# The attention item loop of a two-layer decoder trunk: three engines in source order, and the background work in another order

## The chip, the cores and the metric

The kernel runs on one core of one Trainium2 chip. The metric is the device time of one execution in microseconds. The kernel before took 1172.36 us (median of three runs: 1175.97, 1169.79 and 1172.36). The changed kernel's time is to be compared with that.

## The reference, cut to what matters

A decoder trunk of two layers with S = 512 rows, D = 1024, 16 heads of 64 in 4 groups. Layer A is a short gated convolution and an MLP; then one shared key/value side is projected; layer B is native sparse attention on it, and an MLP. The change touches layer B's attention:

```python
kv = (h @ w_kv).reshape(B, S, 6, N_KV_GROUPS, HEAD_DIM)
k_raw, v_raw, k_sel, v_sel, k_win, v_win = (kv[:, :, i] for i in range(6))
k_cmp = compress_blocks(k_raw, cmp_pe_k, phi_k_w1, phi_k_w2)   # 31 tokens: silu(blocks @ w1) @ w2
v_cmp = compress_blocks(v_raw, cmp_pe_v, phi_v_w1, phi_v_w2)
...
def one_block(qb):                                             # 4 blocks of 128 queries
    o_c = softmax(qt . k_cmp + bias_c) @ v_cmp                 # compressed branch
    o_s = softmax(qt . k_sel + bias_s) @ v_sel                 # selection branch
    o_w = softmax(qt . k_win + bias_w) @ v_win                 # window branch
    return gt[..., 0:1] * o_c + gt[..., 1:2] * o_s + gt[..., 2:3] * o_w
...
x = x + o.reshape(B, S, N_HEADS * HEAD_DIM) @ w_o
x = x + squared_relu_mlp(rms_norm(x, norm_mlp[layer]), mlp_w1[layer], mlp_w2[layer])
```

With 512 rows and 8 selection blocks of 64, all causal blocks are selected and the window reaches over all rows, so both branches are plain causal attention here, each on its own keys and values.

## The kernel before, in words

**Products.** Every large matmul is done in fp16 with each operand split in a high and a low part, in three products (`mm3`, L341 to L343: hi x hi, hi x lo, lo x hi). Weights come from memory in pieces of 128 x 1024 by DMAs on SyncE's queue (`wst`), in the order of the list that begins at L100 and is built by `block` and `cols`; ScalarE makes `whi` (L195) and VectorE `wlo` (L196). `next_piece` takes the next one of the list, `ahead_fine` converts the following ones in steps of 512 columns between the matmuls.

**PSUM.** `bank(name)` gives accumulators in rotation: two each of a, b and c, one each of d and e. In the item loop background pieces use "a" (through `abank`), scores use "b", transposes, the compressed branch's outputs and the finish use "c", and "d" and "e" accumulate PV.

**Items.** The attention stage is a list of 96 items. `Full(g, qb, br, heads)` is one to four heads of group g for query block qb against the keys of one branch (0 selection, 1 window), and `Cmp(gp, qb)` eight heads of two groups against the compressed tokens. List A has the 44 items of groups 0 and 1; B has 22 of group 2 and four Cmp of groups 0 and 1; C has 22 of group 3 and the four Cmp of groups 2 and 3. `mixed(items, extra, start, step)` puts the first Cmp ahead of the item `start` of its list and the others each `step` items further. An item has five steps:
- `st0`: scores into a bank "b" (L954, L955); VectorE adds the bias, finds the row bound and copies to `at_s` (L962, a fused reduce); ScalarE takes exp into `at_p` (L964).
- `st1`: transposes of `at_p` into a bank "c" (L970); ScalarE writes the high part `at_ph` (L973).
- `st2`: VectorE writes the low part `at_pl` (L976).
- `st3`: PV in three products (L989 to L991); for the last head of a branch VectorE scales by the gate and the row sum (`rl`, `add_parts`, L894 and L898, `o_t`), POOL adds into `o` (L900, L903).
- `st4`: when all branches of a group and block are in, `finish` transposes `o` (L917) and splits it into the output operand, which lies in `big`.

`need()` names the background pieces that must be issued before the scores, `need3()` those before PV.

**Background.** A generator hands out the remaining projections in small portions between the items: values of the selection branch (v0), queries of group 1 (q1), keys and values of the window branch (k1, v1), q2, then `raw(0)`, `phi(0)` (compressed keys), `raw(1)`, `phi(1)` (compressed values, marked "cmp"), q3, and, when the outputs of groups 0 and 1 are there ("o1"), the half of the output projection that needs them. Each turn of the loop has a credit; a yield costs the number yielded (0.65 for six matmuls of 512 columns), or 0.1. `ensure(names)` runs the generator until a named piece is done, whatever the credit.
- `gated_pair` accumulates two banks "a" over eight weight slices. `queries` evicts them with L645 (VectorE), then ScalarE and POOL (L746, L747) write `Q`; `keys` evicts with L645 and writes `KD` four times per bank on ScalarE (L691) and VectorE (L693).
- `values` evicts four half banks with ScalarE and L716 on VectorE.
- `raw` evicts with L765 into `at_s`, splits it into `kr_hl` (L362 ScalarE, L364 VectorE; one buffer), and six DMAs per half copy that, shifted, into `big` (L771 to L773, SyncE's queue). `big` has one buffer.
- `phi` multiplies `big` by the first compression weights in 96 matmuls of 155 columns in all, goes through tanh and a multiplication (`phi_t`, L804 to L806, ScalarE and VectorE), splits into `phi_h`, and does a second, small product. For the values that product takes `phi_h` repeated into `kr_hl` (L828, L833) and is evicted into VC by L838 and a split.
- `out_proj` evicts with L469 into the residual `X`.

**Order.** Everything is written in source order, but the Tile scheduler decides the order in which each engine gets its instructions. The loop writes the steps of an item some turns apart:

```python
lead = {1: 2, 2: 3, 3: 4, 4: 6}
...
items[i].st0()
credit += 1.25 if "q3" not in done else 0.9
...                                             # background, while credit > 0
for s in (1, 2, 3, 4): j = i - lead[s]; ...     # st1 of item i-2, st2 of i-3, st3 of i-4, st4 of i-6
```

Before the loop a lead-in issues k0, q0 and the gates, with accumulators of its own choice (`acc`).

Of the kernel before, what the change touches and what calls it, by code (L numbers as in the profile page):

```python
# [10 lines left out]
F32 = mybir.dt.float32  # L11
# [37 lines left out]
def body(ctx, tc, x, rel_bias, norm_mix, norm_mlp, mlp_w1, mlp_w2, a_w_in, a_conv_w, a_w_out,  # L49
# [69 lines left out]
    block(w_kv, 1024)  # L119
    block(w_kv, 1280)  # L120
    block(b_w_qg[0], 512)
    block(w_kv, 0)
    block(phi_k_w1, 0, SW, 0, 16)
# [476 lines left out]
    with pool("attn") as ap:  # L600
# [153 lines left out]
        def raw(which):  # L754
# [7 lines left out]
            for m in range(2):  # L762
                t = ftile("at_s", 3)
                by_stride = lambda a: a.rearrange("p (b r) -> p r b", r=16)
                DVE.tensor_tensor(t.rearrange("p (r b) -> p r b", r=16), by_stride(po[m]), by_stride(rbk),  # L765
                                  op=OP.mult)
                hl = ap.tile([128, 4, S], F16, name="kr_hl", bufs=1)[:, 0:2]
                split_to(hl[:, 0], hl[:, 1], t)
                for s in range(2):
                    g, r = 2 * m + s, slice(64 * s, 64 * s + 64)  # L770
                    nc.sync.dma_start(kr[0:64, :, g, :], hl[r])  # L771
                    nc.sync.dma_start(kr[64:128, :, g, 0:S - 32], hl[r, :, 32:S])
                    nc.sync.dma_start(kr[64:128, :, g, S - 32:S - 1], hl[r, :, 1:32])  # L773
                yield
# [4 lines left out]
        def phi(which):  # L779
# [18 lines left out]
            for m in range(2):  # L798
                bias = ap.tile([128, 2], F32, name="phi_b", bufs=2)
                ACT.activation(bias[:, 0:1], ph[m][:, 124:125], AF.Copy)  # L800
                ACT.activation(bias[:, 1:2], ph[m][:, 124:125], AF.Copy, scale=0.5 / (SW * SK))
                t = ap.tile([128, G, 31], F32, name="phi_t", bufs=2)
                v = ph[m][:, 0:124].rearrange("p (g j) -> p g j", g=4)
# [7 lines left out]
            if which == 0:  # L811
                pk = bank("c")
                w2 = [ap.tile([128, 2, 2, 64], F16, name=f"phi_w2{i}") for i in range(2)]
                for i in range(2):
# [7 lines left out]
            else:  # L822
                pv = bank("c")
                hd = ap.tile([128, 4, S], F16, name="kr_hl", bufs=1).rearrange(
                    "p (m i) (g h n) -> p m i g h n", m=2, g=G, h=4)
                for m in range(2):
                    for i in range(2):
                        DVE.tensor_copy(hd[:, m, i], hs[:, m, i][:, :, None, :].to_broadcast([128, G, 4, 32]))  # L828
                for g in range(4):
                    o = pv[:, g * 64:(g + 1) * 64]  # L830
                    for m in range(2):
                        lh = [hd[:, m, i, g].rearrange("p h n -> p (h n)") for i in range(2)]
                        PE.matmul(o, lh[0], w[0][:, m], start=m == 0, stop=False)  # L833
                        PE.matmul(o, lh[0], w[1][:, m], start=False, stop=False)
                        PE.matmul(o, lh[1], w[0][:, m], start=False, stop=m == 1)
# [36 lines left out]

        for k in (keys(0), marked("q0", queries(0)), gates()):
            drain(k)
# [5 lines left out]
        def add_parts(g, n, qb, src, scale):  # L880


            if (g // 2, qb) not in og:
                og[g // 2, qb] = ap.tile([128, 2, 256], F32, name="o", bufs=6)
            dst = og[g // 2, qb][:, g % 2:g % 2 + n].rearrange("p g (h d) -> p (g h) d", d=64)
# [219 lines left out]
        A = branch(0, 0) + branch(1, 0) + branch(0, 1) + branch(1, 1)  # L1105
        B = mixed(both(2, (0, 1, 2, 3)), [Cmp(0, qb) for qb in range(4)], 10, 3)
        C = mixed(both(3, (3, 2, 1, 0)), [Cmp(1, qb) for qb in (3, 2, 1, 0)], 4, 4)
# [4 lines left out]
        def background():  # L1112
            yield from marked("v0", values(0))
            yield from marked("q1", queries(1))
            yield from marked("k1", keys(1))
            yield from marked("v1", values(1))
            yield from marked("q2", queries(2))
            yield from raw(0)
            yield from phi(0)
            yield from raw(1)  # L1120
            yield from marked("cmp", phi(1))
            yield from marked("q3", queries(3))
            while "o1" not in done:
                yield "wait"
            yield from out_proj(0)
# [8 lines left out]

        lead = {1: 2, 2: 3, 3: 4, 4: 6}
        credit = 0.0
        for i in range(len(items) + 6):
            if i < len(items):
                ensure(items[i].need())
                at_item.get(i, lambda: None)()  # L1140
                items[i].st0()
            credit += 1.25 if "q3" not in done else 0.9
            while credit > 0.0:
                u = next(bg, "end")
                if u in ("wait", "end"):
                    credit = 0.0
                else:
                    credit -= u or 0.1
            for s in (1, 2, 3, 4):
                j = i - lead[s]  # L1150
                if 0 <= j < len(items):
                    if s == 3:
                        ensure(items[j].need3())
                    getattr(items[j], f"st{s}")()
        for _ in bg:
# [147 lines left out]
```

## Time and profile before

| | us |
|---|---|
| median of three runs | 1172.36 |
| lowest, highest run | 1169.79, 1175.97 |
| profiled execution | 1169.18 |
| its span | 1167.4 |
| attention stage, as looked at below (524 to 831) | 307.0 |
| TensorE busy in it | 267.5 |
| VectorE, ScalarE, GpSimd busy in it | 235.7, 201.4, 44.5 |
| mean granted TensorE clock | 0.988 |

The profile is of one execution. PE is TensorE's matmuls, PEld its weight loads, DVE VectorE, ACT ScalarE, POOL GpSimd, SP SyncE. Names such as L976 are lines of the kernel before, and "out<-in" gives tiles by the program's names. A group of instructions has its count, its busy time, the mean duration of one in ns, then the idle time of its engine just before them and what ended it. "Waited for" rows tell, for one engine, the instruction that waited, the one that released it, the sum in us, how often, and the longest. Rows of time stretches give busy time and count for each engine, then the granted clock as a part of full speed, the share of the DMA engines' time, and GB/s.

### The profile page before, as it was taken

Reading aid. Unit: us, or ns where it says so; the run is one execution under the profiler, and the core shown is the slowest. Engines: PE = TensorE matmul, PEld = TensorE weight load, DVE = VectorE, ACT = ScalarE, POOL = GpSimd, SP = SyncE. Lnnn points to the kernel's source line nnn. Section 1 sums busy time; section 2 is a strip of 40 time slices with the busy share of each in tenths; the row PEclk is TensorE's granted clock in tenths of the full one; section 3 lists DMA queues with packets and bytes.
Section 4 is the critical chain, followed back from the end, with each engine's and each line's share of the span. In section 5 each row is a group of like instructions: output and inputs, shape, how many; then the busy total and the mean of one; then the engine's idle time right before and its main releaser. Section 6 shows DMA issues by size and latency. Waiting matters only on the chain.

```text
span 1167.4 us, 20139 instructions
## 1 busy us (share of the span) xinstructions
PE 1103.2 (95%) x7959; PEld 697.5 (60%) x7959; DVE 835.2 (72%) x1527; ACT 571.4 (49%) x924; POOL 159.1 (14%) x201
## 2 busy tenths in 40 slices
PE   9999999999999999998899759799999999999995
PEld 4444444447874468856576636566444688445884
DVE  5755568756986558987687837887976589754795
ACT  4523344444343444467677736665744443343352
POOL 0000001321001220001102000312043200022020
PEclk9999999999999999999999989999999999999998
DMA  6432336333333332242112533011543333330221
GB/s 204 128 104 95 108 98 185 96 109 109 109 110 108 108 98 93 72 129 77 51 56 77 150 89 108 3 53 58 161 128 91 109 113 105 109 108 19 73 91 73
DMA packets 149378, 115.75 MB, mean 99 GB/s; under 512 B 8612, under 2 KB 146564, under 8 KB 149284
## 3 DMA queue, kind: packets, MB, share of 16 engines
q1 hardware_dynamic: 146736, 109.47, 30.8%
q10 hardware_dynamic: 2260, 4.40, 1.2%
q8 instruction: 62, 1.02, 0.3%
q0 software_dynamic: 288, 0.61, 0.2%
q14 instruction: 32, 0.26, 0.1%
HBM read 110.22 MB, written 2.14 MB: 96 GB/s over the span
## 4 chain that ended last, share of the span: by engine, by line
PE 41%; DVE 22%; ACT 13%; issue 9%; POOL 8%; DMA 5%; SPq 1%; DVEq 0%; ACTq 0%; POOLq 0%
POOL ml_z L503 7%; DVE wlo L185 5%; PE a L341 5%; PE a L342 5%; PE a L343 5%; DMA wst<-mlp_w_dram 4%; ACT rh L504 4%; DVE wlo L196 3%; DVE wst L182 3%; DVE ml_t L499 3%; PE b L342 2%; PE b L341 2%; ACT ml_z L501 2%; PE b L343 2%; PE c L341 2%
## 5 line engine op out<-in xcount | busy, mean ns | idle before, releaser
L195 ACT ACTIVATE whi<-wst 128x1024 f16<-128x1024 f32 (+3 forms) x170 | 142.0, 860 | 142.6 <-PE a L342 48.8
L196 DVE SCALAR_TENSOR_TENSOR wlo<-wst,whi 128x1024 f16<-128x1024 f32 (+3 forms) x170 | 167.4, 992 | 54.6 <-ACT whi L195 54.4
L503 POOL TENSOR_TENSOR ml_z<-ml_z 128x256 f32<-128x256 f32 x128 | 102.6, 822 | 602.7 <-ACT ml_z L501 402.7
L341 PEld LDWEIGHTS <-whi 128*128 128x128 f16 x1024 | 101.0, 99 | 126.1 <-issue 16.4
L184 ACT ACTIVATE whi<-wst 128x1792 f16<-128x1792 f32 x64 | 106.8, 1691 | 131.8 <-DVE wst L182 103.1
L343 PEld LDWEIGHTS <-wlo 128*128 128x128 f16 x1024 | 100.7, 98 | 112.3 <-issue 0.8
L342 PEld LDWEIGHTS <-whi 128*128 128x128 f16 x1024 | 100.7, 98 | 107.0 <-issue 1.3
L505 DVE TENSOR_TENSOR rl<-ml_z,rh 128x1792 f16<-128x1792 f32 x32 | 64.8, 2025 | 139.2 <-ACT rh L504 139.2
L185 DVE SCALAR_TENSOR_TENSOR wlo<-wst,whi 128x1792 f16<-128x1792 f32 x64 | 129.4, 2027 | 2.9 <-ACT whi L184 2.9
L182 DVE TENSOR_TENSOR wst<-wst 128x256 f32<-128x256 f32 x256 | 107.0, 460 | 22.2 <-DMA wst<-mlp_w_dram 21.0
L504 ACT ACTIVATE rh<-ml_z 128x1792 f16<-128x1792 f32 x32 | 54.3, 1697 | 106.2 <-POOL ml_z L503 106.2
L552 PEld LDWEIGHTS <-wlo 128*128 128x128 f16 x896 | 87.6, 98 | 14.9 <-issue 3.9
L551 PEld LDWEIGHTS <-whi 128*128 128x128 f16 x896 | 87.6, 98 | 14.5 <-issue 4.0
L550 PEld LDWEIGHTS <-whi 128*128 128x128 f16 x896 | 87.6, 98 | 10.6
L964 ACT ACTIVATE at_p<-at_s,at_m 128x128 f32<-128x128 f32 (+3 forms) x128 | 70.9, 555 | 35.0 <-DVE at_m L962 34.6
L501 ACT ACTIVATE ml_z<-ml_t 128x1024 f32<-128x1024 f32 x32 | 33.8, 1056 | 88.3 <-DVE ml_t L499 88.3
L341 PE MATMUL a<-xsh,whi 128*128 128x512 f16 x192 | 72.8, 379 | 1.9 <-DVE phi_t L806 1.9
L551 PE MATMUL a<-rl,whi 128*128 128x256 f16 x256 | 69.8, 273 | 3.4 <-DVE rl L505 3.4
L341 PE MATMUL c<-xsh,whi 128*128 128x512 f16 x192 | 72.8, 379 | 0.0
L342 PE MATMUL c<-xsl,whi 128*128 128x512 f16 x192 | 72.8, 379 | 0.0
L343 PE MATMUL c<-xsh,wlo 128*128 128x512 f16 x192 | 72.8, 379 | 0.0
L343 PE MATMUL b<-xsh,wlo 128*128 128x512 f16 x192 | 72.8, 379 | 0.0
(309 smaller groups left out, 2719.9 us busy)
## 6 DMA issues: line engine op xcount, KB each, us to landing
wst<-mlp_w_dram SPq DMA_DIRECT2D x256, 256.0 KB, 3.3
wst<-a_w_in_dram SPq DMA_DIRECT2D x18, 512.0 KB, 3.5
wst<-w_kv_dram SPq DMA_DIRECT2D x12, 512.0 KB, 3.6
T<-ext_d ACTq DMA_DIRECT2D x4, 1056.0 KB, 5.3
wst<-a_w_out_dram SPq DMA_DIRECT2D x8, 512.0 KB, 3.4
wst<-b_w_qg_dram SPq DMA_DIRECT2D x8, 512.0 KB, 3.6
wst<-b_w_o_dram SPq DMA_DIRECT2D x8, 512.0 KB, 3.4
wst<-a_w_in_dram SPq DMA_DIRECT2D x8, 384.0 KB, 5.4
```

The source lines that it names most:

```text
L182: DVE.tensor_tensor(b[:, :, o], b[:, :, x], b[:, :, y], op=e)
L184: ACT.activation(hi, b[:, :, 1:], AF.Copy, scale=sc)
L185: DVE.scalar_tensor_tensor(lo, b[:, :, 1:], sc, hi, op0=OP.mult, op1=OP.subtract)
L195: ACT.activation(hi[:, s:e], w, AF.Copy, scale=sc)
L196: DVE.scalar_tensor_tensor(lo[:, s:e], w, sc, hi[:, s:e], op0=OP.mult, op1=OP.subtract)
L341: PE.matmul(ps, w[0], xs[0], start=start, stop=False)
L342: PE.matmul(ps, w[0], xs[1], start=False, stop=False)
L343: PE.matmul(ps, w[1], xs[0], start=False, stop=stop)
L503: POOL.tensor_tensor(z[:, o], z[:, a], z[:, b], op=e)
L504: ACT.activation(rh[0][:, p], z[:, 1:8], AF.Copy)
L550: PE.matmul(acc7[i], wh, xh, start=c == 0 and not other, stop=False, skip_group_check=other)
L551: PE.matmul(acc7[i], wh, xl, start=False, stop=False, skip_group_check=other)
```

## The change: three engines in source order, and the background rearranged

In words: (1) the loop stands in a block in which TensorE, ScalarE and VectorE take their instructions in the order of the source; GpSimd and SyncE are left to the scheduler. (2) Each turn writes finish of item i-6, PV of i-4, transposes of i-2, scores of i, low part of i-2, then background with credits of 1.3 and 0.85; before that it asks for what item i+2 needs. (3) v0 moves to the lead-in. (4) raw(0) comes ahead of q2 (with its weights, `block(w_kv, 0)`), and four turns without further background ("rest") stand between raw(1) and phi(1). (5) `kr_hl` has two buffers of half the size, and the copies of the second half of each pair go to GpSimd's queue. (6) The first Cmp stands at item 58 in place of 54, and they follow every third in place of every fourth. (7) `o` has seven buffers, paid with one buffer of `phi_t` and with tiles that the second compression product now takes from others.

```diff
@@ weights
+    block(w_kv, 0)
     block(b_w_qg[0], 512)
-    block(w_kv, 0)
@@ raw
-                hl = ap.tile([128, 4, S], F16, name="kr_hl", bufs=1)[:, 0:2]
+                hl = ap.tile([128, 2, S], F16, name="kr_hl", bufs=2)
                 split_to(hl[:, 0], hl[:, 1], t)
                 for s in range(2):
                     g, r = 2 * m + s, slice(64 * s, 64 * s + 64)
-                    nc.sync.dma_start(kr[0:64, :, g, :], hl[r])
-                    nc.sync.dma_start(kr[64:128, :, g, 0:S - 32], hl[r, :, 32:S])
-                    nc.sync.dma_start(kr[64:128, :, g, S - 32:S - 1], hl[r, :, 1:32])
+                    q = (nc.sync, nc.gpsimd)[s]
+                    q.dma_start(kr[0:64, :, g, :], hl[r])
+                    q.dma_start(kr[64:128, :, g, 0:S - 32], hl[r, :, 32:S])
+                    q.dma_start(kr[64:128, :, g, S - 32:S - 1], hl[r, :, 1:32])
@@ phi
-                t = ap.tile([128, G, 31], F32, name="phi_t", bufs=2)
+                t = ap.tile([128, G, 31], F32, name="phi_t", bufs=1)
...
-                w2 = [ap.tile([128, 2, 2, 64], F16, name=f"phi_w2{i}") for i in range(2)]
+                w2 = [ap.tile([128, S], F16, name=n, bufs=3)[:, 0:256].rearrange("p (m a b) -> p m a b", m=2, a=2)
+                      for n in ("at_ph", "at_pl")]
...
-                hd = ap.tile([128, 4, S], F16, name="kr_hl", bufs=1).rearrange(
-                    "p (m i) (g h n) -> p m i g h n", m=2, g=G, h=4)
+                hd = [ap.tile([128, 2, S], F16, name="kr_hl", bufs=2).rearrange(
+                    "p i (g h n) -> p i g h n", g=G, h=4) for _ in range(2)]
@@ lead-in, lists, background
-        for k in (keys(0), marked("q0", queries(0)), gates()):
+        for k in (keys(0), marked("q0", queries(0)), gates(), marked("v0", values(0))):
...
-                og[g // 2, qb] = ap.tile([128, 2, 256], F32, name="o", bufs=6)
+                og[g // 2, qb] = ap.tile([128, 2, 256], F32, name="o", bufs=7)
...
-        B = mixed(both(2, (0, 1, 2, 3)), [Cmp(0, qb) for qb in range(4)], 10, 3)
+        B = mixed(both(2, (0, 1, 2, 3)), [Cmp(0, qb) for qb in range(4)], 14, 2)
...
-            yield from marked("v0", values(0))
             yield from marked("q1", queries(1))
             yield from marked("k1", keys(1))
             yield from marked("v1", values(1))
+            yield from raw(0)
             yield from marked("q2", queries(2))
-            yield from raw(0)
             yield from phi(0)
             yield from raw(1)
+            for _ in range(4):
+                yield "rest"
             yield from marked("cmp", phi(1))
@@ the loop
-        lead = {1: 2, 2: 3, 3: 4, 4: 6}
-        for i in range(len(items) + 6):
-            if i < len(items):
-                ensure(items[i].need())
-                at_item.get(i, lambda: None)()
-                items[i].st0()
-            credit += 1.25 if "q3" not in done else 0.9
-            while credit > 0.0:
-                u = next(bg, "end")
-                if u in ("wait", "end"):
-                    credit = 0.0
-                else:
-                    credit -= u or 0.1
-            for s in (1, 2, 3, 4):
-                j = i - lead[s]
-                if 0 <= j < len(items):
-                    if s == 3:
-                        ensure(items[j].need3())
-                    getattr(items[j], f"st{s}")()
+        with tc.manual_schedule(engines={mybir.EngineType.PE, mybir.EngineType.Activation, mybir.EngineType.DVE}):
+            for i in range(len(items) + 6):
+                def step(n, k):
+                    if 0 <= i - k < len(items):
+                        it = items[i - k]
+                        if n == 3:
+                            ensure(it.need3())
+                        getattr(it, f"st{n}")()
+                if i < len(items):
+                    ensure(items[min(i + 2, len(items) - 1)].need())
+                    ensure(items[i].need())
+                    at_item.get(i, lambda: None)()
+                step(4, 6)
+                step(3, 4)
+                step(1, 2)
+                step(0, 0)
+                step(2, 2)
+                credit += 1.3 if "q3" not in done else 0.85
+                while credit > 0.0:
+                    u = next(bg, "end")
+                    if u in ("wait", "end", "rest"):
+                        credit = 0.0
+                    else:
+                        credit -= u or 0.1
```

More of the change, by code (lines that the diff above doesn't have):

```diff
@@ L823, in phi @@
                 pv = bank("c")
-                hd = ap.tile([128, 4, S], F16, name="kr_hl", bufs=1).rearrange(
-                    "p (m i) (g h n) -> p m i g h n", m=2, g=G, h=4)
+                hd = [ap.tile([128, 2, S], F16, name="kr_hl", bufs=2).rearrange(
+                    "p i (g h n) -> p i g h n", g=G, h=4) for _ in range(2)]
                 for m in range(2):
                     for i in range(2):
-                        DVE.tensor_copy(hd[:, m, i], hs[:, m, i][:, :, None, :].to_broadcast([128, G, 4, 32]))
+                        DVE.tensor_copy(hd[m][:, i], hs[:, m, i][:, :, None, :].to_broadcast([128, G, 4, 32]))
                 for g in range(4):
@@ L831, in phi @@
                     for m in range(2):
-                        lh = [hd[:, m, i, g].rearrange("p h n -> p (h n)") for i in range(2)]
+                        lh = [hd[m][:, i, g].rearrange("p h n -> p (h n)") for i in range(2)]
                         PE.matmul(o, lh[0], w[0][:, m], start=m == 0, stop=False)
```

## The prediction

> **What bounds the kernel now.** I read the page first, then the busy time by stage, then what TensorE waited for, last the groups of the engines that release it.
>
> ```profile
> PE 1103.2 (95%) x7959; PEld 697.5 (60%) x7959; DVE 835.2 (72%) x1527; ACT 571.4 (49%) x924; POOL 159.1 (14%) x201
> ```
>
> TensorE is busy for 95% of the profiled execution, so a change of order can only win back idle TensorE time. The diff touches the attention stage alone, 524 to 831 us. Busy time there (us, PE, PEld, DVE, ACT, POOL, each with its count; then granted clock, DMA share, GB/s):
>
> ```profile
> 524.00:535.00 11.00, 8.04 (x74) 6.32 (x72) 8.28 (x24) 9.45 (x22) 4.95 (x4) 1.00 0.15 49
> 535.00:560.00 25.00, 24.89 (x216) 16.65 (x214) 19.44 (x53) 17.73 (x46) 0.30 (x1) 1.00 0.28 86
> 560.00:567.00 7.00, 4.00 (x36) 2.12 (x35) 2.15 (x13) 3.85 (x11) 4.96 (x4) 1.00 0.23 75
> ...
> 640.00:660.00 20.00, 15.11 (x185) 11.21 (x184) 17.25 (x60) 15.47 (x50) 1.46 (x2) 0.91 0.50 134
> ...
> 684.00:699.00 15.00, 1.88 (x42) 1.66 (x41) 3.98 (x6) 2.35 (x4) 0.00 (x0) 0.68 0.44 105
> 699.00:728.00 29.00, 26.72 (x258) 19.33 (x256) 20.81 (x59) 16.60 (x45) 1.47 (x2) 0.93 0.29 92
> 728.00:757.00 29.00, 22.86 (x265) 16.75 (x266) 25.28 (x61) 20.17 (x45) 9.62 (x9) 0.94 0.06 19
> ...
> sum 307.00, PE 267.52 PEld 184.32 DVE 235.74 ACT 201.39 POOL 44.50; mean PE 20.58 PEld 14.18 DVE 18.13 ACT 15.49 POOL 3.42
> ```
>
> The stage holds 307.0 - 267.5 = 39.5 us of idle TensorE; nothing the change does can win more, the half clock (0.68 and 0.91 to 0.94) aside. VectorE, at 235.7 of 307, is next: 77% over the stage, 87% in 728 to 757. What the idle time waited for (us, times, longest):
>
> ```profile
> PE a L341 <- DMA big<-kr_hl: 13.1, 1, 13.1
> PE b L954 <- POOL Q L747: 4.7, 7, 1.1
> PE a L341 <- DVE phi_t L806: 3.7, 2, 1.9
> PE c L970 <- DVE at_pl L976: 3.7, 6, 1.7
> PE d L989 <- ACT at_ph L973: 3.2, 5, 1.4
> PE b L1027 <- DVE at_m L962: 2.0, 1, 2.0
> PE b L954 <- DVE at_m L962: 1.6, 2, 0.9
> ...
> PE a L341 <- DVE VT L716: 0.3, 1, 0.3
> ```
>
> One wait is a third of it: phi(1) cannot start before the raw copies have landed. The last row matters for what follows: today a projection that needs a bank just being evicted costs next to nothing, since items are pulled ahead of it.
>
> **The change part by part.** Gains first.
>
> Start of the loop: 524 to 535 idles 2.96 us. With v0 drained before the loop, its 96 matmuls run with nothing beside them but lose nothing (they depend only on weights), and Q of group 0 is older by them. I leave 1.0 us: -2.0. From 560 to 567 3.00 us are idle while POOL is busy for 4.96 of 7: the items of a group stand behind the Q that POOL is still writing. With items two slots ahead asked for early, the pair is finished sooner: -3.0.
>
> 640 to 660 idles 4.89 us, and its clock of 0.91 costs about 0.09 x 15.11 = 1.4 us more; VectorE is full there (17.25 of 20) because raw, a Cmp and conversions meet. Spread out, about 1.5 stay: -4.8.
>
> The at_pl, at_ph and at_m waits add up to 10.5 us in the rows above; some 6.5 lie in 640 to 660 and 728 to 757. With two slots between the steps the other 4 should vanish: -4.0. From 728 to 757 no background is left; 6.14 us are idle, but VectorE itself needs 25.28 of the 29, so 3.7 is the most: -2.0.
>
> The raw copies. The second half (m = 1) waited for the first half's copies, kr_hl being one buffer:
>
> ```profile
> 683.51 1.97 DVE L765 TENSOR_TENSOR at_s<-a,rb 128x512 f32<-128x512 f32 x2 [2.62 <-PE a L343]
> ...
> 686.76 0.60 SPq L771 DMA_DIRECT2D big<-kr_hl  x1
> ...
> 691.96 0.63 ACT L362 ACTIVATE kr_hl<-at_s 128x512 f16<-128x512 f32 x1 [6.24 <-DMA big<-kr_hl]
> ...
> 698.49 0.29 PE L341 MATMUL a<-big,whi 128*128 128x155 f16 x1 [13.12 <-DMA big<-kr_hl]
> ...
> 707.25 0.23 PE L343 MATMUL a<-big,wlo 128*128 128x155 f16 x1
> 709.30 0.38 PE L341 MATMUL a<-xqh,whi 128*128 128x512 f16 x1 [1.81 <-DVE phi_t L806]
> ...
> 711.64 0.10 PEld L833 LDWEIGHTS <-kr_hl 128*128 128x128 f16 x1 [0.24 <-DVE kr_hl L828]
> ```
>
> Two buffers take the 6.24 us out of the chain, and two queues halve the issuing. But in source order the changed program splits and copies in slot 54 (a slot is one turn of the loop), and slot 56 asks for Cmp (first at 58, two ahead): all of phi(1) is then due at once. Only two of the four rests act, some 2 us of item work, by these rows of a slot:
>
> ```profile
> 633.01 0.49 PE L970 MATMUL c<-ident,at_p 128*128 128x128 f32 x3
> ...
> 634.01 0.38 PE L341 MATMUL a<-xsh,whi 128*128 128x512 f16 x1
> ...
> 635.31 0.49 PE L970 MATMUL c<-ident,at_p 128*128 128x128 f32 x3
> ```
>
> From the transposes to the background 1.0 us of items, then 1.3 of six products, to the next transposes. Landing on POOL's queue is not in the trace for these copies; the nearest rows:
>
> ```profile
> rb<-final_norm_dram POOLq DMA_DIRECT2D x2, 256.0 KB, 3.7
> ...
> big<-kr_hl SPq DMA_DIRECT2D x8, 128.0 KB, 2.4
> ```
>
> A landing there is bounded by 2.4 and 3.7; I take 3.7, the row of that queue. From the end of the projection to the last landing: L765 twice 1.97, the splits of both halves 2 x (0.63 + 0.68), three issues of 0.60 on one queue, landing 3.7, and the reduce and at_pl of two slots ahead of them on VectorE, 2 x 1.1: 12.3, of which the 2 are covered. 13.1 becomes some 10.4: -2.7 (bounds: -11, nearly all covered, if VectorE is free sooner and all four rests act; +4, the POOL queue's rival below). Nothing else stands behind these copies: POOL's Q subtractions of q3 come later, and SP's weights are spared three issues per half. raw(0)'s copies have all of q2 (slots 33 to 40) to land in. Together -18.5.
>
> On the clock: 684 to 699 stands at 0.68, 699 to 728 at 0.93. The Trainium skill (TensorE: Matmul & The Clock Gate, What's actually happening) says that the gate watches a free-running window of about 3.4 us and that one idle window halves the clock; a wait still of 10 us keeps whole idle windows, so by it nothing is won back here, and without it at most 0.4 us; the sum takes nothing.
>
> Now the losses. In order, TensorE stands at the first matmul of a background piece until its bank "a" (two buffers) is evicted, and VectorE has that eviction behind the slot's reduce (L962) and at_pl (L976):
>
> ```profile
> L196 DVE SCALAR_TENSOR_TENSOR wlo<-wst,whi 128x512 f16<-128x512 f32 x60 | 40.8, 698 | 8.2 <-ACT whi L195 8.1
> L976 DVE SCALAR_TENSOR_TENSOR at_pl<-c,at_ph 128x512 f16<-128x512 f32 x56 | 38.5, 687 | 8.8 <-ACT at_ph L973 8.4
> L962 DVE CUSTOM_DVE_ANT_0 at_s<-b,T 128x512 f32<-128x512 f32 x32 | 21.8, 681 | 0.0
> L976 DVE SCALAR_TENSOR_TENSOR at_pl<-c,at_ph 128x384 f16<-128x384 f32 x32 | 17.6, 551 | 6.7 <-ACT at_ph L973 6.7
> L962 DVE CUSTOM_DVE_ANT_0 at_s<-b,T 128x384 f32<-128x384 f32 x32 | 17.6, 551 | 0.9 <-PE b L955 0.6 <-PE a L707 0.2
> L962 DVE CUSTOM_DVE_ANT_0 at_s<-b,T 128x256 f32<-128x256 f32 x32 | 12.2, 416 | 1.4 <-PE b L955 1.4
> ...
> L645 DVE TENSOR_TENSOR at_s<-a,rb 128x512 f32<-128x512 f32 x8 | 5.2, 682 | 0.0
> L765 DVE TENSOR_TENSOR at_s<-a,rb 128x512 f32<-128x512 f32 x4 | 3.9, 1024 | 2.6 <-PE a L343 2.6
> L716 DVE SCALAR_TENSOR_TENSOR VT<-a,rtok,VT 128x256 f16<-128x256 f32 x8 | 3.7, 477 | 0.1
> L693 DVE TENSOR_TENSOR KD<-at_s,KD 64x512 f16<-64x512 f32 x4 | 2.7, 687 | 0.3 <-ACT KD L691 0.2
> ...
> L691 ACT ACTIVATE KD<-at_s 64x512 f16<-64x512 f32 x4 | 2.5, 625 | 0.0
> ```
>
> q1 ends its matmuls in slot 7 with the credit spent; its evictions follow slot 8's reduce and at_pl, and k1's first matmul follows slot 8's scores: 0.68 + 0.55 + 0.68 = 1.9 us. In the same way k1 to v1, slot 16: 0.55 + 0.55 + 0.68 = 1.8; v1 to raw(0), slot 24, two reduces of 0.42, at_pl, two VT, less one covered product step of 0.33: 2.2; raw(0) to q2, slot 32, 0.68 + 0.69 + 1.02 - 0.65 = 1.7; q2 to phi(0), slot 40, 0.68 + 0.55 + 0.68 - 0.65 = 1.3; out_proj(0), whose banks L469 (0.68) evicts, slots 79, 85 and 91: 2.2, 1.8, 1.5 by the size of the item there. Sum 14.4. The bounds are 0.3 each (the VT row), 2.4 in all, and 14.4; I take the upper, for the order leaves TensorE nothing else to take.
>
> k1's tail puts on VectorE at once two L645 and eight KD (0.687 each), with two waits for ACT of 0.63: 8.1 us, then three conversions of 0.70, and only then slot 17's reduce and at_pl: with the two before it 12.4 us after slot 16's scores. TensorE has 7.4 us until PV needs that at_pl (three backgrounds of 1.3, three slots' items of 1.0 and part of a fourth): 5.0 lost, with all later items queued behind that PV; lower bound 0, if VectorE is let run ahead.
>
> phi's tail runs between two slots, phi_t now one buffer, so its second half waits for the first. After phi(0) products stand behind it: +1.1. After phi(1) TensorE has nothing until 711.64 - 707.5 = 4.1 where 1.8 was idle: +2.3. VC's evictions: four groups of three passes of 256 elements at 0.42 = 5.0 on VectorE, against some 1.6 slots of TensorE's 2.3, 3.75: +1.3. Lower bound of the three together 0.
>
> Losses 14.4 + 5.0 + 1.1 + 2.3 + 1.3 = 24.1. At nothing stand `o` at seven buffers (a wait on o_t or `o` is about a microsecond now), w2 in the at_ph slots (same copies) and the piece order of w_kv (it follows use; POOL and SP have room). Sum: 24.1 - 18.5 = +5.6, so 1174.8 against the profiled execution's 1169.18, of which what lies outside the stage stays. The runs' median, 1172.36, stands 3.2 above it, the lowest run 0.6: I add 2.2, between the two: **1177**.
>
> **The rivals.** *Faster.* The waits at bank "a" come with VectorE near idle, and what the two slots of distance free flows on: losses stay at their low ends, 2.4 for evictions and half of k1's (2.5), and the rests cover phi(1)'s copies (-11 instead of -2.7). Then gains of 26.8 against losses of 4.9: 1169.2 - 21.9 = 1147, and 1150 at the median. For it: 24.89 of 25 in 535 to 560 shows that an order can hide a projection's tail; against: there the order was free to put items ahead. It decides as soon as losses fall under 18.5.
>
> *Slower, VectorE compounding.* After each tail VectorE is late, its next reduce is late, and with 77% load it regains only 0.23 us per us; three bursts (k1, raw, phi) each lose as k1 does, 5.0 more twice: 1187. Decides where a tail exceeds the 7.4 us of cover. For: 17.25 of 20 busy at 640; against: two slots' distance.
>
> *Slower, the POOL queue starves.* Copies issued from POOL wait whenever VectorE works. While phi(1) waits (684 to 699) VectorE is busy for 3.98 us, so at most about 4 are added there; raw(0)'s are covered by q2: 1177 + 4 = 1181. For it: POOL's own 3.7 against SP's 2.4; against: that row is twice as large. The Trainium skill (SBUF — State Buffer, SBUF: two separate sides) speaks against the change here: descriptors of a DMA issued by GpSimd cannot be written while VectorE runs an operation that holds the shared port pair. No run here shows it so far.
>
> *No effect.* The rests are cut short by slot 56, the scheduler's order was already near this one: 1172.
>
> **How the numbers follow.** Within 0.5% is 1166.5 to 1178.2, about what a measurement of this kernel can tell from no change. Forecast 0.42 (own range 1168 to 1188: 0.27 slower, 0.13 same, 0.02 faster), faster rival 0.37, compounding 0.11, POOL starving 0.05, no effect 0.05. Faster 0.39, same 0.18, slower 0.43. The range runs from the faster rival's 1150 to 1194, all of the losses and none of the gains (1169.2 + 24.1 = 1193.3).
>
> **What would show it.** Right: waits of 1 to 2 us of L341 on bank "a" released by L645, L716 and the raw scaling at each change of piece; a gap of some 5 us after k1; a wait on big<-kr_hl of 8 to 11 us; none left on POOL Q. Wrong: that DMA wait under 4, the bank waits under 0.5 each, or TensorE idle in the stage under 25 us; then the faster rival holds. A wait over 15 us on the copies points to POOL's queue.

## The result: slower by 5.2%, and the profile after

| | median us | runs | ratio to before, 95% interval |
|---|---|---|---|
| before (the three runs above and one more) | 1171.49 | 4 | |
| changed | 1232.48 | 4 (1230.45 to 1238.33) | 1.0517 [1.0475, 1.0559] |

The profiled execution of the changed kernel took 1238.33 us, its span is 1236.6 us. That is 69.2 us longer than the span of the kernel before (1167.4): 62 of them lie between the first scores and the last finish, 6 ahead of that, and 1 behind it (354.6 us against 353.4). The rows below give that stretch as time windows (length; busy time and count of PE, PEld, DVE, ACT, POOL; granted clock; DMA share; GB/s). The kernel before:

```profile
528.00:814.00 286.00, 247.74 (x2553) 174.35 (x2552) 217.41 (x628) 186.71 (x494) 42.89 (x51) 0.96 0.24 72
```

The changed kernel:

```profile
534.00:882.00 348.00, 263.43 (x2489) 179.64 (x2487) 225.51 (x626) 189.41 (x488) 45.76 (x60) 0.88 0.19 57
```

It grew by 62 us although it has 64 matmuls fewer (those of v0 that stood in it), and starts 6 us later with v0 ahead of it. Idle TensorE time went from 38.3 to 84.6 us (+46.3), and TensorE's busy time rose by 15.7 with fewer matmuls: the clock is down from 0.96 to 0.88. These are two prices, one for standing still and one for a slower pace.

What TensorE waited for in the changed kernel (line and tile, releaser, us in all, times, longest); lines past 770 stand two or less further on than in the kernel before:

```profile
PE c L341 <- DVE at_ph L818: 13.4, 1, 13.4
PE a L341 <- DMA big<-kr_hl: 11.3, 1, 11.3
PE e L993 <- DVE at_pl L978: 8.2, 4, 2.3
PE c L972 <- DVE rlc L1071: 7.7, 5, 2.7
PE a L341 <- DVE X L469: 6.9, 3, 3.4
PE c L1066 <- DVE big L364: 4.7, 3, 3.4
PE d L993 <- DVE at_pl L978: 4.4, 2, 3.2
PE a L341 <- DVE VT L716: 4.3, 2, 3.3
PE c L835 <- DVE kr_hl L830: 4.2, 1, 4.2
PE c L972 <- DVE at_pl L978: 3.7, 6, 1.3
PE a L341 <- DVE at_s L645: 3.3, 3, 1.9
PE a L341 <- DVE at_s L765: 3.0, 2, 2.8
PE e L991 <- ACT at_ph L975: 3.0, 1, 3.0
...
PE a L706 <- DVE at_s L645: 1.7, 1, 1.7
```

The waits on POOL's Q (4.7 us before) are gone; almost every other releaser is VectorE, which is hardly busier than before (225.5 against 217.4 us). The first row is the largest; it is phi(0)'s tail, which the prediction's sum has at 1.1. VectorE's timeline shows what is inside it (start, us, what ran, in brackets the idle time before it and its releaser):

```profile
680.23 1.29 DVE L196 SCALAR_TENSOR_TENSOR wlo<-wst,whi 128x512 f16<-128x512 f32 x2 [1.06 <-ACT whi L195]
687.81 0.27 DVE L628 COPY Tc<-T 128x128 f32<-128x128 f32 x1 [6.28 <-DMA T<-ext_d]
687.99 0.28 DVE L964 CUSTOM_DVE_ANT_0 at_s<-b,T 128x128 f32<-128x128 f32 x1
...
691.00 0.35 DVE L807 SCALAR_TENSOR_TENSOR phi_t<-a,phi_b,phi_t 128x124 f32<-128x124 f32 x1 [1.40 <-ACT phi_t L806]
691.72 0.29 DVE L366 SCALAR_TENSOR_TENSOR phi_h<-phi_t,phi_h 128x124 f16<-128x124 f32 x1 [0.38 <-ACT phi_h L362]
692.93 0.35 DVE L807 SCALAR_TENSOR_TENSOR phi_t<-a,phi_b,phi_t 128x124 f32<-128x124 f32 x1 [0.92 <-ACT phi_t L806]
```

`load_T` writes the copy into Tc right behind the DMA that brings T. In source order VectorE stands at that copy until the DMA has landed, 6.28 us, while scores, phi's tail and the products behind it queue up. At 653.37 the same happens for T of group 2 (3.59 us). In the kernel before, whose order the scheduler chose, the copies into Tc waited for their DMAs for 0.9 us in all.

### The profile page after: what moved, and what is told of

Same layout as the page of the kernel before. It is cut to its first block, busy times and chain, and to the rows that moved or that the text cites. A ratio compares the mean times of both kernels' runs of the same rounds, so it can differ in the third digit from the quotient of the medians.

```text
span 1236.6 us, 20220 instructions
## 1 busy us (share of the span) xinstructions
PE 1126.8 (91%) x7959; PEld 709.9 (57%) x7959; DVE 848.4 (69%) x1527; ACT 576.9 (47%) x924; POOL 166.7 (13%) x213
## 4 chain that ended last, share of the span: by engine, by line
PE 49%; DVE 21%; ACT 11%; issue 8%; DMA 5%; POOL 5%; SPq 0%; DVEq 0%; ACTq 0%; POOLq 0%
POOL ml_z L503 5%; PE a L341 4%; PE a L342 4%; PE a L343 4%; DVE wlo L196 4%; DMA wst<-mlp_w_dram 3%; DVE wlo L185 3%; ACT rh L504 3%; PE b L342 3%; PE b L341 3%; PE b L343 3%; PE c L343 2%; PE c L341 2%; PE c L342 2%; PE c L972 2%
## 5 line engine op out<-in xcount | busy, mean ns | idle before, releaser
L196 DVE SCALAR_TENSOR_TENSOR wlo<-wst,whi 128x1024 f16<-128x1024 f32 (+3 forms) x170 | 170.2, 1013 | 71.0 <-ACT whi L195 70.8
L503 POOL TENSOR_TENSOR ml_z<-ml_z 128x256 f32<-128x256 f32 x128 | 99.9, 802 | 605.9 <-ACT ml_z L501 406.4
L966 ACT ACTIVATE at_p<-at_s,at_m 128x128 f32<-128x128 f32 (+3 forms) x128 | 71.2, 557 | 72.7 <-DVE at_m L964 72.6
L964 DVE CUSTOM_DVE_ANT_0 at_s<-b,T 128x128 f32<-128x128 f32 (+3 forms) x128 | 59.2, 486 | 34.6 <-PE b L957 34.4
L342 PE MATMUL a<-xsl,whi 128*128 128x512 f16 x192 | 74.0, 386 | 0.0
L343 PE MATMUL a<-xsh,wlo 128*128 128x512 f16 x192 | 74.0, 385 | 0.0
L341 PE MATMUL b<-xsh,whi 128*128 128x512 f16 x192 | 72.7, 379 | 0.3 <-DVE X L469 0.3
```

The costliest lines, as they stand in the source:

```text
L196: DVE.scalar_tensor_tensor(lo[:, s:e], w, sc, hi[:, s:e], op0=OP.mult, op1=OP.subtract)
L341: PE.matmul(ps, w[0], xs[0], start=start, stop=False)
L342: PE.matmul(ps, w[0], xs[1], start=False, stop=False)
L343: PE.matmul(ps, w[1], xs[0], start=False, stop=stop)
L503: POOL.tensor_tensor(z[:, o], z[:, a], z[:, b], op=e)
```

## The experiments

All times are medians, each beside runs of the kernel before on the same chip; a saving against the changed kernel is the difference of the ratios times 1171.5.

**Order or arrangement.** Two kernels split the change in two: one has all of it but the fixed order, the other has the changed loop with its fixed order on the old lists, background and copies.

```diff
# e1_sched, from the changed kernel
-        with tc.manual_schedule(engines={PE, Activation, DVE}):
+        if True:
# e2_loop, from the kernel before
-        lead = {1: 2, 2: 3, 3: 4, 4: 6}
-        (its loop)
+        (the changed loop, with tc.manual_schedule)
```

> The changed kernel without the block that fixes the order; lists, background, copies and buffers stay changed. Theory A (the fixed order costs the time: an instruction of VectorE that waits holds up all behind it, and TensorE has nothing else to take): 1160 to 1180 us. Rival B (the rearranged background, Cmp and copies cost it): 1215 us or more. Half each would be about 1200.

> The kernel before with the changed loop alone (fixed order on three engines, distances, credits, asking two items ahead); background order, lists, copies and buffers as before. Theory A: 1215 to 1250 us. Rival B: within 1% of before, 1160 to 1185 us.

Measured: 1156.19 us, ratio 0.9858 [0.9833, 0.9883], and 1252.20 us, ratio 1.0672 [1.0650, 1.0694]. Both came out on theory A's side, each a little beyond its range (1160 to 1180, 1215 to 1250): the arrangement alone is a gain of 16.6 us, and fixing the order of the very same work costs 77. The stretch from first scores to last finish without the fixed order:

```profile
534.00:801.00 267.00, 241.83 (x2481) 168.72 (x2480) 215.99 (x622) 185.12 (x486) 48.04 (x60) 0.96 0.25 74
```

Beside the changed kernel's 348 us with the same instructions, 81 us are to be explained: idle time 25.2 against 84.6 (59.4), busy time 241.8 against 263.4 (21.6). The clock column fits the second: if the clock stands at 0.5 or 1, as in the windows further down, 0.88 over 348 us is an estimated 84 us at half clock, 0.96 over 267 us some 21. In the second kernel the wait for the raw copies is 30.4 us in two places, in the first 5.8 in one.

**The same loop under the scheduler.**

```diff
# e12_sched_loop, from e2_loop
-        with tc.manual_schedule(engines={PE, Activation, DVE}):
+        if True:
```

> The kernel before with the changed loop alone (distances, credits, asking two items ahead) under the scheduler, no fixed order. With the order fixed the same text took 1252. Theory A: the text of the loop is nearly neutral, 1165 to 1180, and the fixed order costs 70 to 85 us here too. If the distances and the look-ahead carry the gain of 17 us: 1162 or less.

Measured: 1175.04 us, ratio 1.0010 [0.9996, 1.0025]. So the loop's distances, credits and look-ahead are worth nothing measurable to the scheduler, and the fixed order costs the same 78 us (1.0672 - 1.0010) on the old arrangement as on the new one.

**Which engine's order.** From the changed kernel, with the order fixed for some engines only:

```diff
-        with tc.manual_schedule(engines={PE, Activation, DVE}):
+        with tc.manual_schedule(engines={PE}):                  # e3_pe
+        with tc.manual_schedule(engines={PE, DVE}):             # e5_pe_dve
+        with tc.manual_schedule(engines={PE, Activation}):      # e5_pe_act
+        with tc.manual_schedule(engines={Activation, DVE}):     # e5_dve_act
```

> The changed kernel with the order fixed for TensorE alone; ScalarE and VectorE are left to the scheduler. Theory A1 (TensorE's fixed order is what costs): 1215 us or more. Theory A2 (VectorE's and ScalarE's fixed order costs: blocked heads such as the copy Tc behind its DMA, tails of eight KD and splits ahead of at_pl): 1170 to 1195 us.

> The changed kernel with the order fixed for TensorE and VectorE, ScalarE left to the scheduler. With TensorE alone it took 1182, with all three 1232. If VectorE's fixed order makes the other 50 us (its instructions wait for a DMA or for ScalarE and hold up the next reduce and at_pl): 1215 us or more. If ScalarE's does: 1195 or less.

> The changed kernel with the order fixed for TensorE and ScalarE, VectorE left to the scheduler. If VectorE's fixed order makes the 50 us: 1195 us or less. If ScalarE's does (exp and at_ph behind the weight conversions of the slot): 1215 or more.

> The changed kernel with the order fixed for VectorE and ScalarE, TensorE left to the scheduler. Without any fixed order 1156, TensorE alone 1182, all three 1232. If the costs add up (26 for TensorE, 50 for the other two): some 1206 us. If a blocked VectorE hurts only because TensorE may not take anything else: 1175 or less. If TensorE's freedom is worth nothing once VectorE is in order: 1220 or more.

| order fixed for | us | ratio to before, interval | against no fixed order |
|---|---|---|---|
| none | 1156.19 | 0.9858 [0.9833, 0.9883] | |
| TensorE | 1182.15 | 1.0074 [1.0057, 1.0091] | +25 |
| TensorE, ScalarE | 1189.10 | 1.0141 [1.0088, 1.0194] | +33 |
| TensorE, VectorE | 1209.37 | 1.0299 [1.0253, 1.0344] | +52 |
| ScalarE, VectorE | 1201.20 | 1.0225 [1.0196, 1.0255] | +43 |
| all three | 1232.48 | 1.0517 [1.0475, 1.0559] | +77 |

TensorE's order is the smaller part: 25 us alone, 34 on top of the other two. VectorE and ScalarE in order cost 43 even where TensorE may take what it likes, 5 us under the 1206 expected if costs add up. To TensorE's order VectorE adds 26 and ScalarE 8 (the intervals touch), both together 52. So the run with ScalarE came out on VectorE's side, as expected for VectorE as the cause, but the run with VectorE fell between its two expectations (1195 and 1215): 18 us appear only with both. A reading of the source that no run tests apart: the two chain, for at_pl and VectorE's other low parts wait for ScalarE's high part, exp for VectorE's bound, each behind whatever its engine has ahead. With TensorE free (order fixed for VectorE and ScalarE) the waits change places, to the scores and PV:

```profile
PE b L956 <- DVE at_m L964: 15.9, 11, 5.4
PE e L991 <- ACT at_ph L975: 7.5, 4, 5.0
PE c L972 <- DVE at_pl L978: 7.3, 7, 2.2
PE d L991 <- ACT at_ph L975: 4.7, 5, 1.8
```

None of these is a projection's bank; those behind the evictions of L765 and L716 are 0.8 and 0.5 us there. A free TensorE still runs out of work that is ready.

**Mends within the fixed order.** Four edits of the changed kernel, each against one of its waits, and all four together.

```diff
# e4_tc: the copies into Tc 9 and 19 turns after their DMA
-            DVE.tensor_copy(TC[g // 2][:, g % 2], t[:, :, 0:512:16])          # in load_T, for g >= 2
+        at_item = {..., len(A) + 2: lambda: copy_Tc(2), len(A) + 20: lambda: copy_Tc(3)}
# e6_evict: a pair's evictions in the turn that ends its matmuls (also in values, keys, queries, raw, out_proj)
-                        yield 0.65
+                        if (k, m) != (7, 1):
+                            yield 0.65
# e8_cbank: in finish and in Cmp.st3
-            p = bank("c")
+            p = bank("a" if "q3" in done and "o1" not in done else "c")
# e7_clock: before phi's products
+            if which == 1:
+                for _ in range(30):
+                    PE.matmul(ph[0], KD[:, 0, 0, 0, 0:128], KD[:, 0, 0, 0, :], start=True, stop=True)
```

> The changed kernel with the two copies into Tc (L628) issued 9 and 19 turns after their DMA in place of right behind it, nothing else. If a VectorE instruction that waits for its DMA (3.6 and 6.3 us in the profile) holds up TensorE in full: 10 us less than the changed kernel, some 1221, or up to 13 less with the clock that the gap costs. If TensorE has other waits behind it anyway (phi's tail): under 4 us less, 1228 or more.

> The changed kernel with every eviction of a background pair issued in the turn that ends its matmuls, one turn earlier, so ahead of the next turn's reduce and at_pl on VectorE. The forecast's eviction waits (14.4 us in eight places, of which some 1.2 each are the reduce and at_pl) would fall by 1.2 in nine places: 8 to 14 us less than the changed kernel, 1218 to 1224. If the wait only moves on to scores or PV: under 4 less, 1228 or more.

> The changed kernel, but from the end of q3 until out_proj starts (turns 64 to 72) the compressed items' output and the finish take banks a, idle there, in place of c, which the transposes share. The profile has 12 us of TensorE waits on banks c behind rlc (L1071) and the finish's split (L364), in and after that stretch. If the two banks c in fixed order make them: 4 to 10 us less than the changed kernel, 1222 to 1228. If VectorE is the limit there: within 2 us of it.

> The changed kernel with 30 matmuls of 512 columns (6.5 us at full clock) ahead of phi(1)'s first product, into the bank that this product overwrites: work that nothing uses, inside the wait of 11.3 us for the raw copies. If the gap's half clock costs what the pace of phi(1)'s products after it shows (0.13 us apart, with windows at 0.74): 2 to 5 us less than the changed kernel, 1227 to 1230. If TensorE's pace does not set the end there: no change, or some us more.

> The changed kernel with four mends in the fixed order together: Tc copies late, evictions a turn earlier, banks a in turns 64 to 72, the 30 idle matmuls. Taken singly the first three gave about 8, 22 and 4 us. If these waits are separate: 1195 to 1203 us. If one wait stands behind another: 1208 or more. If the fixed order were sound once its heads are mended: 1165 or less.

| | us | ratio to before, interval | saved, us |
|---|---|---|---|
| Tc late | 1224.86 | 1.0446 [1.0425, 1.0466] | 8 |
| evictions a turn earlier | 1212.12 | 1.0331 [1.0287, 1.0375] | 22 |
| banks a for c | 1229.50 | 1.0485 [1.0435, 1.0534] | 4, not clear of 0 |
| idle matmuls | 1232.66 | 1.0502 [1.0478, 1.0526] | 2, not clear of 0 |
| all four | 1200.79 | 1.0231 [1.0211, 1.0251] | 34 |

*Tc.* Of 9.9 us waited for the two DMAs, 8 came back. TensorE's wait ahead of phi(0)'s second product fell from 13.4 to 8.2 us; what is left is phi's own chain (the copy of L818 stands at L822 in this kernel):

```profile
PE c L341 <- DVE at_ph L822: 8.2, 1, 8.2
```

*Evictions.* The changed order had put a pair's eviction behind the next turn's reduce and at_pl. Moved ahead of them, the waits on L469 fell from 6.9 to 0.3 us and those on L645 vanished. It gave more than the 8 to 14 expected: between first scores and last finish idle time fell by 13.4 (84.6 to 71.2), and busy time by another 4.6 with the clock at 0.91 in place of 0.88. The waits ahead of phi(0)'s second product (13.4 to 11.1) and of phi(1) (11.3 to 9.7) fell too, and behind the last finish the profiled span is 5.5 us shorter (349.1 against 354.6). The row of that stretch:

```profile
534.00:864.00 330.00, 258.82 (x2516) 179.05 (x2514) 225.83 (x631) 188.25 (x488) 44.96 (x59) 0.91 0.20 61
```

*Banks.* The wait moved on rather than away: on c behind rlc it fell from 7.7 to 3.1, but PV's wait on bank d rose from 4.4 to

```profile
PE d L993 <- DVE at_pl L978: 8.4, 5, 3.4
```

*Idle matmuls.* The wait for the raw copies is no longer idle, 2.3 us of it left, but nothing was gained, and why stands in two lists. TensorE's timeline of this kernel:

```profile
715.86 6.65 PE L785 MATMUL a<-KD 128*128 128x512 f16 x30 [2.21 <-DVE at_s L765]
724.82 0.23 PE L341 MATMUL a<-big,whi 128*128 128x155 f16 x1 [2.31 <-DMA big<-kr_hl]
```

and its windows of 1 us behind them (the number behind the five counts is the granted clock):

```profile
724.00:725.00 1.00, 0.18 (x3) 0.21 (x4) 0.00 (x0) 0.00 (x0) 0.00 (x0) 0.99 0.87 236
725.00:726.00 1.00, 1.00 (x11) 1.00 (x9) 0.00 (x0) 0.00 (x0) 0.00 (x0) 0.50 1.00 308
726.00:727.00 1.00, 1.00 (x11) 1.00 (x9) 0.00 (x0) 0.00 (x0) 0.00 (x0) 0.50 0.91 296
727.00:728.00 1.00, 1.00 (x10) 1.00 (x9) 0.00 (x0) 0.12 (x1) 0.00 (x0) 0.50 0.54 184
728.00:729.00 1.00, 1.00 (x14) 1.00 (x13) 0.29 (x1) 0.19 (x1) 0.00 (x0) 0.80 0.05 6
```

The rest of the gap, 2.3 us, was enough to halve the clock for 3.4 us, so phi(1)'s first products ran at half pace all the same. The price of that gap's clock was therefore not measured; only that filling 6.65 of its 11.3 us is no remedy.

*All four* save 34 us, close to the sum (36), and leave 1200.79 us: 44 us above the same work without the fixed order. The largest waits left are phi(0)'s chain (8.7) and at_pl before PV (14.3 in eleven places).

**Where the arrangement's 17 us come from.** Under the scheduler, with the loop of the kernel before or the changed one:

```diff
# e10_copies, from the kernel before: kr_hl bufs=2, second half's copies on gpsimd; nothing else
# e15_bg, from the kernel before: v0 in the lead-in, raw(0) and its weights ahead of q2, rests, Cmp 14, 2,
#   o bufs=7 (the later Cmp need them), phi_t bufs=1, w2 in at_ph and at_pl; nothing else
# e17_bg_copies: both
# e13_rest, from the changed kernel without fixed order (e1_sched)
-                    ensure(items[min(i + 2, len(items) - 1)].need())
```

> The kernel before with the raw copies alone changed: kr_hl in two buffers, the second half of each pair on GpSimd's queue. The forecast gave them 2.7 us, and bounds of -11 to +4. If they carry the gain of the arrangement under the scheduler (17 us): 1160 to 1166 us. If POOL's queue starves: 1176 or more. Otherwise within 3 us of before.

> The kernel before (scheduler, its own loop and copies) with the changed lists and background: v0 in the lead-in, raw(0) ahead of q2 with its weights, the rests, the Cmp from item 58 on, and the seven buffers of o that the later Cmp need, with phi_t and w2 as changed. If these carry the arrangement's gain of 17 us: 1155 to 1165 us. If only all parts together do: 1166 or more.

> As the run with lists and background alone, and the raw copies changed too (two buffers, two queues): all of the change but the loop. If the copies are worth more where the rests cover them: 1150 to 1158 us, at or under the changed kernel without its fixed order. If their 2 us is all: 2 us under the run without them.

> The changed kernel without the fixed order and without asking two items ahead, so that all four rests stand between raw(1) and phi(1). The run with the look-ahead still waited 5.8 us for the copies. If the look-ahead cuts that cover short: 3 to 6 us less, 1150 to 1153. If the scheduler places phi(1) by readiness anyway: 1154 to 1159.

| | us | ratio to before, interval |
|---|---|---|
| copies alone | 1170.88 | 0.9985 [0.9970, 0.9999] |
| lists, background, buffers alone | 1160.78 | 0.9887 [0.9856, 0.9918] |
| both | 1155.29 | 0.9833 [0.9798, 0.9867] |
| all but the fixed order, no look-ahead | 1156.56 | 0.9853 [0.9818, 0.9888] |

The lists and the background carry it (13 us), the copies add 6 on top of it and 2 alone. Which of the list's parts carries the 13 us was not taken apart. With the copies alone TensorE waits for them 13.7 us in two places (13.1 in the kernel before), with the lists alone 10.0, with both

```profile
PE a L341 <- DMA big<-kr_hl: 3.6, 1, 3.6
```

The look-ahead made no difference to the scheduler; the 3 to 6 us that dropping it might have saved did not come. The version with lists, background and copies, the old loop and no fixed order beats both kernels: 1155.29 us, 1.7% under the kernel before. It cannot be told from the run of all but the fixed order.

## Why the prediction was wrong

It forecast 1177 us, gave slower 0.43, and closed its range at 1194 with "all of the losses and none of the gains". The sign was the likelier one; the size was off by 55 us. Between the same work without the fixed order and the changed kernel lie 59.4 us of idle time, where the sum of losses has 24.1, and 21.6 us of longer work, where it has nothing; and gains were taken off that the fixed order did not leave. (The range's upper end, 1193.3, also lacks the 2.2 us that the forecast adds for the median; that decides nothing here.)

- **Most of the listed waits came about as priced.** Eviction waits, forecast 14.4 us in eight places, were 19.2 (the rows of L469, L716, L645 and L765 above; largest 3.4, 3.3 and 2.8 where 2.2, 2.2 and 1.7 were forecast). k1's burst, forecast 5.0, was 3.0 + 2.3 in PV's waits. The wait for the copies, forecast 10.4, was 11.3. phi(1)'s tail, forecast 4.1, was 4.2. Reading the changed source order slot by slot with durations from the trace gives such waits to within a few us. phi(0)'s tail is the exception, below.
- **Failed step 1: "the sum takes nothing" for the clock.** TensorE is busy for 21.6 us longer than without the fixed order for the same instructions. The prediction asked only whether the long gap of phi(1) would keep its half clock, and not what the new gaps of 2 to 3 us would do. At one of them, v1 to raw(0), TensorE's timeline reads

```profile
611.24 0.59 PE L341 MATMUL a<-xsh,whi 128*128 128x512 f16 x1 [3.28 <-DVE VT L716]
```

and the windows of the same kernel are at half clock from 610.4 to 617.2 (612.00 to 617.00 below, first and last):

```profile
612.00:613.00 1.00, 1.00 (x12) 0.68 (x11) 0.85 (x2) 0.60 (x2) 0.00 (x0) 0.50 0.00 0
...
616.00:617.00 1.00, 1.00 (x4) 0.39 (x3) 0.25 (x2) 0.79 (x3) 0.00 (x0) 0.50 0.00 0
```

Of these 6.8 us 0.8 lie in the gap itself, so the gap of 3.3 us costs up to half of the other 6.0, 3.0 us: the price of this wait is nearly double. Not every gap has that price (last section); over the whole stretch 59.4 us of idle time came with 21.6 of longer work, 0.36 us per us.
- **Failed step 2: VectorE's queue was walked only where an eviction or a tail stands in it.** For the copies into Tc the part "the change part by part" had no term: an instruction that the diff does not touch, but that gets a new place, since now nothing may pass it. It cost 8 us. phi(0)'s tail, priced at 1.1, was 13.4, and is still 8.2 with those copies moved away: its chain runs over both engines, with the next slot's reduce and at_pl ahead of its last copy. The waits on banks c behind rlc and the finish's split (7.7 and 4.7) had no term either. The prediction asked what stands behind a waiting TensorE, and not the same of every DMA and ScalarE wait of VectorE. The table by engine shows the weight of that: 25 us for TensorE's order alone, 52 more for the other two.
- **Failed step 3: gains were booked that the fixed order took away.** Of the waits on at_pl, at_ph and at_m 4.0 us "should vanish" with two slots between the steps, and 2.0 were to be won in the stretch without background. The waits of PV and the transposes on at_pl alone went from 4.3 us (two rows here, and 3.7 on banks c in the prediction's list) to 16.3:

```profile
PE e L991 <- DVE at_pl L976: 0.4, 1, 0.4
PE d L991 <- DVE at_pl L976: 0.2, 1, 0.2
```

  The loop's distances are worth nothing under the scheduler either (1175.04 us, ratio 1.0010). And the stretch with the compressed items, where the prediction saw VectorE as the limit, takes 58 us in place of 42 for nearly the same VectorE work (before first, then after):

```profile
715.00:757.00 42.00, 35.39 (x381) 24.51 (x379) 37.64 (x99) 28.85 (x68) 11.09 (x11) 0.96 0.08 26
```

```profile
754.00:812.00 58.00, 41.99 (x395) 27.54 (x393) 38.41 (x95) 27.73 (x61) 11.48 (x12) 0.85 0.09 28
```

  Idle there went from 6.6 to 16.0 us. The Q waits went (4.7 us, forecast 3.0), and the wait for the copies fell by 1.8 (forecast 2.7).
- **A gain of that size exists, but without the fixed order:** 18.5 us were forecast, 16.6 measured without it (19.6 with the old loop). That the sums are so near is in part luck, for the parts differ. Without the fixed order the waits for the copies and for Q fell by 7.3 and 4.4 us, where 2.7 and 3.0 were forecast, and those of the scores on at_m rose from 1.6 to 6.0, where they were to fall:

```profile
PE b L956 <- DVE at_m L964: 6.0, 5, 3.1
PE a L341 <- DMA big<-kr_hl: 5.8, 1, 5.8
PE b L956 <- POOL Q L747: 0.3, 1, 0.3
```

  The mistake was to add these gains to the fixed order's losses as if independent.
- **The rivals.** "VectorE compounding" had the right engine and sign at 1187; what it lacked is that the burst of k1 is not the only kind of head: DMA waits and ScalarE's half of each pair count too. "POOL starves" did not happen: the copies on POOL's queue landed in 3.5 and 3.6 us where SyncE's took 3.0 and 4.3, though VectorE was busy for 6.04 of the 10 us from 720 to 730. The Trainium skill's rule on descriptors held back by VectorE (SBUF — State Buffer, SBUF: two separate sides) thus had no effect that can be seen here; whether VectorE ran an operation that holds the shared ports is not shown:

```profile
big<-kr_hl SPq DMA_DIRECT2D x4, 128.0 KB, 3.0
big<-kr_hl POOLq DMA_DIRECT2D x4, 128.0 KB, 3.5
big<-kr_hl SPq DMA_DIRECT2D x4, 120.0 KB, 4.3
big<-kr_hl POOLq DMA_DIRECT2D x4, 120.0 KB, 3.6
```

  The faster rival fell with the result; a gain of that kind shows only without the fixed order (1156.19 us). The first sentence of the prediction's bound, that TensorE's 39.5 us of idle time limit the gain, stood; it says nothing of the loss.

Open: how the remaining 44 us of the mended kernel divide between the chain of phi(0), at_pl behind ScalarE, and the clock. The clock's 21.6 us are measured as longer busy time; no run held the clock up with the waits left in place.

## What to carry to other kernels

Fixing the order of an engine turns every instruction that may wait, also one that the diff leaves alone, into a wait of everything behind it. So before an engine is put in source order, walk its whole queue for DMA waits, waits for another engine's half of a pair, and tails of several instructions, and price each gap with what the clock may lose behind it (here 0.36 us per us on the whole). Try a rearrangement and a fixed order apart: here one gave 17 us and the other took 77, and only together did the change look like a plain loss.

## What the runs showed of the hardware

A gap of TensorE need not be long to halve the clock, and its length alone does not decide: 2.31 us without a matmul (722.5 to 724.8 in the kernel with idle matmuls, with work on both sides) was followed by 3.4 us at 0.50, and one of 3.28 us by half clock from 610.4 to 617.2. In the changed kernel a gap of 1.86 us ahead of k1, at 556.6, left the clock at 1.00, and one of 1.88 us ahead of PV, at 671.5, was followed by 0.50. The clearest pair is one and the same gap, raw(0) to q2, in the changed kernel and in the kernel with idle matmuls, which differ only further on. In the changed kernel:

```profile
636.24 0.39 PE L341 MATMUL a<-xqh,whi 128*128 128x512 f16 x1 [2.78 <-DVE at_s L765]
...
636.00:640.00 4.00, 3.53 (x39) 2.34 (x40) 2.61 (x5) 2.10 (x4) 1.82 (x3) 1.00 0.26 65
```

In the kernel with idle matmuls:

```profile
634.91 0.39 PE L341 MATMUL a<-xqh,whi 128*128 128x512 f16 x1 [2.78 <-DVE at_s L765]
...
636.00:640.00 4.00, 4.00 (x28) 2.43 (x26) 3.30 (x13) 2.17 (x6) 2.97 (x5) 0.57 0.51 127
```

So whether a short gap halves the clock changes from one execution to another; what decides it was not tested. The Trainium skill (TensorE: Matmul & The Clock Gate, What's actually happening) ties the drop to an idle window of about 3.4 us. The stretches of 3.4 and 6.8 us at half clock agree with steps of that length, but here gaps shorter than such a window were enough.
